# Both feed-forward layers of a transformer block as seven half products per pair of tiles, with weight sums formed by adding transfers

## The chip, the cores and the metric

The kernel runs on one core of a Trainium2 chip. Times are device microseconds (us) of one execution on that core. The engines are named as the profile names them: PE (matrix products), PEld (the loading of weights into PE, beside its products), DVE (vector), ACT (scalar, with its functions), POOL (general purpose) and SP, which here only starts transfers. SP, ACT and POOL each have a queue from which they issue DMA transfers. Every engine works through its own list of instructions in a fixed order; an instruction that waits holds up all that stand behind it on the same engine.

## What is computed

One block of a model on 640 tokens (128 context tokens, 512 latent ones), width 1024: a norm, two kinds of attention, an output projection, a second norm, a feed-forward net of hidden width 4096, and a last norm. The change touches the part from the second norm on:

```python
def _mlp(h, w_mlp_in, w_mlp_out):
    return jnp.square(jax.nn.relu(h @ w_mlp_in)) @ w_mlp_out
...
    x = x + g1 * _merge(a_o, b_o, ga, gb, w_br_a, w_br_b, w_out)
    h2 = _rmsnorm(x, n2) * (1 + sc2) + sh2
    x = x + g2 * _mlp(h2, w1, w2)
...
y_prompt = _rmsnorm(xp, final_norm_g)
```

The gates g, scales sc and shifts sh are a product of the conditioning vectors with a 1024 x 6144 matrix.

## The kernel before

Features lie on the 128 partitions, tokens along the free dimension: an activation is 8 tiles of 128 x 640, a weight tile is 128 output features by 1024 inputs (8 blocks of 128 x 128). Tokens are worked in two halves of 320. To keep float32 accuracy each operand is split into a high and a low part in a faster format: ACT writes the high part (a copy that rounds), DVE or POOL writes the low part (the difference). Each product is then three matmuls of 128 x 128 with 128 x 320: high by high, high by low, low by high (`gemm_k`, L339 to L341).

The hidden width is done in four chunks of 1024. In each chunk a first layer makes 8 hidden tiles (relu, then square, `relu2`, L1140 to L1150), and a second layer multiplies them with the chunk's 8 tiles of the second matrix and adds the result, scaled by the gate, to the residual tiles X1 (`add_gated`, L1100). A plain tile and token half takes 8 blocks x 3 = 24 matmuls. The first layer of chunk 0 and all second layers are plain. The first layers of chunks 1 to 3 take two weight tiles at a time as a 2 x 2 block matrix (input features 0 to 511 and 512 to 1023 by two tiles) and multiply it with the two token halves by seven products of half the depth, 12 matmuls each, in place of eight (`winograd`, L1204). The operands of the seven are the blocks A11, A12, A22 themselves and sums of blocks, S1 to S4, which DVE forms in SBUF (`raw`, L260) from two weight tiles that are held whole; ACT and DVE or POOL then split each (L280, L281). The sums on the activations' side, three sets T and a fourth that takes H2's place, are formed once from the normed input, in pieces between the products of chunk 0's second layer (`t_pieces`).

The order of DVE's list is that in which the program is written, from the merge before the output projection on (`manual_schedule`); those of PE, ACT, POOL and SP are set by the scheduler that builds the program. The output projection runs its last four tiles with the first token half ahead, so that the second norm of that half can run beside the second half's products. The norm's pieces are popped from the list `side` in the midst of and behind the products that follow: `rstd_half` (PE sums over the partitions, L174 and L175, then ACT, L176 and L177), then `norm2`, which scales (DVE, L360), shifts into the high part (ACT, L365) and makes the low part (DVE, L368). The second half's pieces run beside chunk 0's first products, which take the first token half of four weight tiles.

The gates, scales and shifts but the first norm's come from `late_mods`: 32 loads of 512 KB on POOL's queue (tiles wmt), and for each load four reductions on DVE (L992). `mod_pace` and `mod_step` put these between the products from the merge to chunk 0's first layer; the last eight loads, for the gates of the feed-forward net, come last.

## Time and profile before

| what | value |
|---|---|
| time, three runs | 1003.18, 1004.53, 1004.98 us (median 1004.53) |
| the profiled execution | span 1001.3 us, from the first to the last instruction; no time of its own is listed |
| feed-forward net in the profile | first product at 545.03 us, last at 991.27 us |
| ACT busy in 870 to 925 us (chunk 3, first layer) | 29.80 us of 55 |
| DVE busy in the same stretch | 40.55 us of 55 |

The profile's page counts the busy time of each engine over the span. Its other views list instructions in order of time, groups of like instructions with the mean duration of one and the wait ahead of it, busy times by stretches of the span, and transfers with the time from issue to landing. A matmul is listed with its whole passage through the array (0.31 us), which overlaps with the next one's; the distance between two starts is what one costs PE in a row of them.

### The profile page before, as it was taken

How to read it: one execution, taken by the hardware profiler on the slowest of the kernel's cores; microseconds unless marked ns; L12 is line 12 of the kernel's file. 1: busy time of each engine (PE TensorE's matmuls, PEld its weight loads, DVE VectorE, ACT ScalarE, POOL GpSimd, SP SyncE). 2: the span in 40 equal slices, each digit the busy share in tenths (PEclk: the TensorE clock that was granted, in tenths of full speed). 3: DMA queues.
4: the chain of work that ended last, by engine and by line, in shares of the span. 5: the costliest groups of instructions: out<-in, count | busy, mean ns of one | idle time of the engine just before them, and what ended most of it. 6: DMA issues, size and time to landing. Idle time of an engine off the chain costs nothing.

```text
span 1001.3 us, 16554 instructions
## 1 busy us (share of the span) xinstructions
...
## 2 busy tenths in 40 slices
...
GB/s 347 208 172 69 31 25 44 77 43 77 135 111 103 133 160 189 181 169 185 224 126 81 47 164 110 85 43 84 106 78 28 85 106 88 60 79 29 126 22 105
DMA packets 34767, 108.47 MB, mean 108 GB/s; under 512 B 4320, under 2 KB 8032, under 8 KB 34688
## 3 DMA queue, kind: packets, MB, share of 16 engines
...
## 4 chain that ended last, share of the span: by engine, by line
PE 65%; DVE 15%; ACT 8%; issue 3%; DMA 1%; POOL 0%; ACTq 0%; DVEq 0%; POOLq 0%; SPq 0%
PE pg L339 7%; PE pg L340 7%; PE pg L341 7%; PE pss L340 7%; PE pss L341 7%; PE pss L339 6%; PE pt L339 4%; PE pt L341 4%; PE pt L340 4%; DVE sr L260 3%; ACT wb L280 2%; PE pt L653 1%; PE pt L710 1%; DMA wst<-w 1%; DVE n L641 1%
## 5 line engine op out<-in xcount | busy, mean ns | idle before, releaser
L301 ACT ACTIVATE wh<-wst 128x1024 fp32r<-128x1024 f32 x84 | 88.8, 1057 | 112.4 <-PE pg L340 37.9
L302 DVE TENSOR_TENSOR wl<-wst,wh 128x1024 fp32r<-128x1024 f32 x53 | 64.8, 1223 | 67.5 <-ACT wh L301 67.4
L302 POOL TENSOR_TENSOR wl<-wst,wh 128x1024 fp32r<-128x1024 f32 x31 | 75.1, 2423 | 160.0 <-ACT wh L301 151.5
L992 DVE SCALAR_TENSOR_TENSOR mt<-wmt,cb 128x512 f32<-128x512 f32 x128 | 81.4, 686 | 0.0
L281 POOL TENSOR_TENSOR wb<-wst,wb 128x512 fp32r<-128x512 f32 x24 | 31.7, 1322 | 263.4 <-ACT wb L280 226.6
L339 PE MATMUL pss<-hidh,wh 128*128 128x320 f32 x216 | 67.0, 310 | 0.7 <-ACT hidh L1143 0.7
L340 PE MATMUL pss<-hidl,wh 128*128 128x320 f32 x216 | 67.0, 310 | 0.3
L341 PE MATMUL pss<-hidh,wl 128*128 128x320 f32 x216 | 66.7, 309 | 0.0
L607 DVE TENSOR_TENSOR pl<-pt,ph 128x512 fp32r<-128x512 f32 (+2 forms) x80 | 50.5, 633 | 18.3 <-ACT ph L606 17.3
L606 ACT ACTIVATE ph<-pt 128x512 fp32r<-128x512 f32 (+2 forms) x80 | 44.2, 555 | 28.8 <-PE pt L710 11.7
L280 ACT ACTIVATE wb<-sr 128x512 fp32r<-128x512 f32 x48 | 29.8, 627 | 51.5 <-DVE sr L260 35.6
L1150 DVE TENSOR_TENSOR hidl<-rl,hidh 128x320 fp32r<-128x320 f32 x64 | 37.5, 586 | 25.2 <-ACT hidh L1143 24.6
L988 POOL DMA_DIRECT2D wmt<-wmodB x32 | 17.1, 536 | 174.6 <-DVE mt L992 108.0
L340 PE MATMUL pg<-hidl,wh 128*128 128x320 f32 x144 | 44.7, 310 | 2.2 <-DVE hidl L1150 2.2
L281 DVE TENSOR_TENSOR wb<-sr,wb 128x512 fp32r<-128x512 f32 x48 | 36.0, 755 | 14.2 <-ACT wb L280 14.1
L339 PE MATMUL pg<-hidh,wh 128*128 128x320 f32 x144 | 44.7, 310 | 0.0
L341 PE MATMUL pg<-hidh,wl 128*128 128x320 f32 x144 | 44.5, 309 | 0.0
L340 PE MATMUL pt<-hidl,wh 128*128 128x320 f32 x136 | 42.1, 310 | 1.1 <-DVE hidl L1150 1.1
L341 PE MATMUL pt<-hidh,wl 128*128 128x320 f32 x136 | 42.0, 309 | 0.0
L339 PE MATMUL pt<-hidh,wh 128*128 128x320 f32 x136 | 42.0, 309 | 0.0
L644 ACT ACTIVATE pa<-pss,nm 128x320 f32<-128x320 f32 x64 | 33.1, 522 | 17.2 <-DVE nm L642 17.0
L339 PEld LDWEIGHTS pss<-hidh,wh 128*128 128x128 f32 x216 | 40.5, 188 | 1.5 <-ACT hidh L1143 1.5
...
## 6 DMA issues: line engine op xcount, KB each, us to landing
wst<-w SPq DMA_DIRECT2D x64, 512.0 KB, 3.6
wmt<-wmodB POOLq DMA_DIRECT2D x32, 512.0 KB, 4.2
wst<-w_in SPq DMA_DIRECT2D x31, 512.0 KB, 3.6
ms<-wmodA SPq DMA_DIRECT2D x16, 512.0 KB, 8.8
...
wst<-w_br SPq DMA_DIRECT2D x8, 512.0 KB, 4.4
wst<-w_out SPq DMA_DIRECT2D x8, 512.0 KB, 3.5
```

The source lines that it names most:

```text
L280: ACT.activation(t[:, lo4], src, AF.Copy)
L281: later.append(lambda: (nc.gpsimd if name in BLKP else DVE).tensor_sub(t[:, hi4], src, r32(t[:, lo4])))
L301: ACT.activation(hi, st, AF.Copy)
L302: (nc.gpsimd if key in WPOOLSET else DVE).tensor_sub(lo, st, r32(hi))
L339: PE.matmul(ps, wh[:, k], xh[:, sl], start=first, stop=False)
L340: PE.matmul(ps, wh[:, k], xl[:, sl], start=False, stop=False)
L341: PE.matmul(ps, wl[:, k], xh[:, sl], start=False, stop=last)
L606: ACT.activation(ph[:, :n], pt[:, :n], AF.Copy)
L607: DVE.tensor_sub(pl[:, :n], pt[:, :n], r32(ph[:, :n]))
L644: ACT.activation(p[:, HALVES[j]], ps[j][:, :HT], AF.Exp, bias=nm, accum_out=s2[:, j:j + 1])
L992: DVE.scalar_tensor_tensor(t, st[:, q * 512:(q + 1) * 512], 1.0, r32(cb[2 * q + i][:, :512]), op0=OP.mult, op1=OP.mult, accum_out=parts[:, ...
L1150: DVE.tensor_sub(dst[1][:, sl], r[:, :HT], r32(dst[0][:, sl]))
```

## The change

Both layers of all four chunks are done by seven products of half the depth. On the second layer the 2 x 2 blocks are the halves of the hidden features and two output tiles. A pair of weight tiles n (two tiles of 128 outputs) gives the seven products A11, A12, S3, S2, A22, S1, S4, each 12 matmuls (now L1386 to L1388); some of them add to one bank of PSUM: A12 goes on the bank of A11, S1 and S4 on that of S2, after what was there has been read.

- **Operands of the weights.** Whole weight tiles are loaded only for the A11 and A12 of chunk 0's first layer. All others come as blocks of 256 KB into 12 buffers `ra` (L1177, SP's queue). The sums are made by transfers that add into a buffer (`accum_op`, on POOL's queue): S3 is A21 with A11 added (L1179); S2, S4 and S1 come from S3 and A22 by one more addition each (L1203), issued when the operand before has been split from the same buffer. DVE's sums of blocks are gone. Six split operands can stand ready, as before.
- **Operands of the activations.** They are sets of four tiles, 128 x 1280, formed and split in one instruction per step (`form`, `split_set`). The normed input gives B11, B21 from the first token half (within `norm2`) and T3, T2, T4, T1, N22 once the second half is there. Each chunk's hidden tiles give the same seven for its second layer, into two buffers `op` that take turns.
- **Second layer.** Chunks 0 to 2 don't touch the residual. Each product's result is added to one of 28 sums `acc` (ACT copies in chunk 0, DVE adds in 1 and 2). In chunk 3 `fold` combines the sums and `reload` fetches the residual, which was stored to HBM before the net (`xd`), and adds the sums to it; chunk 3's own products are added one by one, and the last norm's squares are taken tile by tile (`done_half`).
- **Order.** DVE's list is hand-written only up to the end of the second norm; from there the scheduler sets it. Before the second half's norm all reductions of `late_mods` that are left are done (`mod_step(64 - lm_n[0])`), and their buffers are given back; the second norm is drained (`while side`) before the net's first product is written. PSUM is then laid out anew as 8 equal banks. The first products are A11 and A12 of two pairs at a time, which take the first token half only.

```diff
--- before.py
+++ after.py
...
-        def block(self, name, i):
...
-    if MAN:
-        ctx.enter_context(tc.manual_schedule(engines={(DVE.engine, ACT.engine, PE.engine)[i] for i in MAN}))
+    manual = ExitStack()
+    manual.enter_context(tc.manual_schedule(engines={DVE.engine}))
...
+    def split_set(t, src, ks=slice(0, 4), neg=False):
+        hi, lo = halves_of(t)
+        if neg:
+            ACT.activation(hi[:, ks], src[:, ks], AF.Copy, scale=-1.0)
+            DVE.scalar_tensor_tensor(lo[:, ks], src[:, ks], -1.0, r32(hi[:, ks]), op0=OP.mult, op1=OP.subtract)
+        else:
+            ACT.activation(hi[:, ks], src[:, ks], AF.Copy)
+            DVE.tensor_sub(lo[:, ks], src[:, ks], r32(hi[:, ks]))
+    def form(raw, name, tile_of, ks=slice(0, 4)):
+        c = {"B11": B11, "B21": B21, "N22": B22, "T4": B21}.get(name, B12)
+        b = [t[:, ks] for t in raw]
+        if name == "T3":
+            DVE.tensor_sub(b[B12], b[B22], b[B12])
+        elif name == "T2":
+            DVE.tensor_add(b[B12], b[B12], b[B11])
+        elif name == "T4":
+            DVE.tensor_sub(b[B21], b[B21], b[B12])
+        elif name == "T1":
+            DVE.tensor_sub(b[B12], b[B22], b[B12])
+        split_set(tile_of(name), raw[c], ks, name == "N22")
...
     def norm2(fs, h):
         mod_step(16 + 4 * (fs.stop + -fs.stop % MG) - lm_n[0])
-        modulate([(H2[f], X1[f], mod(2, f), mod(1, f)) for f in fs], rstd2, h)
+        off = HALVES[h].start
+        for f in fs:
+            for sl, g in SEGS[h]:
+                d = HR[2 * (f // 4) + h][:, f % 4, sl.start - off:sl.stop - off]
+                DVE.scalar_tensor_tensor(d, X1[f][:, sl], mod(2, f)[:, g:g + 1], rstd2[:, sl], op0=OP.mult, op1=OP.mult)
+                ACT.activation(d, d, AF.Identity, bias=mod(1, f)[:, g:g + 1])
+        if fs.stop % 4 == 0 and h == 0:
+            form(HR, ("B11", "B21")[fs.stop // 4 - 1], h2_set)
...
-        if n < KT - 4 or h == 0 and n < KT - 1:
+        if h or n < KT - 4:
             mod_pace(OU)
-        elif n == KT - 1:
+        if n == KT - 1:
+            if h == 0:
+                HR += [tt_pair("hr", F32).rearrange("p a (b n) -> p (a b) n", b=2) for _ in range(4)]
+            else:
+                mod_step(64 - lm_n[0])
             side += norm_pieces(acc2, sq, rstd2, h, lambda fs, h=h: norm2(fs, h))
-    def t_pieces(k):
...
-    def winograd(i, hid):
...
-    for c in range(4):
-        hid = [(v_tile("hidh"), v_tile("hidl")) for _ in range(KT)]
...
     while side:
         side.pop(0)()
+    for n in range(KT):
+        nc.sync.dma_start(xd[n], X1[n])
+    manual.close()
+    mod_pool.close()
...
+    for name in ("T3", "T2", "T4", "T1", "N22"):
+        form(HR, name, h2_set)
+    banks.close()
+    pp8 = ctx.enter_context(tc.tile_pool(name="pp8", bufs=1, space=bass.MemoryType.PSUM, reuse_waits="tile"))
...
+    m = open_phase("mlp", 0)
+    opt = [m.tile([P, 8, HT], F32R, tag="op", bufs=2, name="op")]
...
+    ORDER = ("A11", "A12", "S3", "S2", "A22", "S1", "S4")
+    def products():
+        for c in range(4):
+            late_ = []
+            if c == 0:
+                first = [(o, n) for i in (0, 2) for o in ORDER[:2] for n in (i, i + 1)]
+                for o, n in first + [(o, n) for o in ORDER[2:] for n in range(4)]:
+                    yield 1, c, n, o
+            else:
+                for n in range(4):
+                    yield 1, c, n, "S3"
+                    if n:
+                        yield 1, c, n - 1, "S1"
+                    yield 1, c, n, "A22"
+                    yield 1, c, n, "A11"
+                    if n:
+                        yield 1, c, n - 1, "S4"
+                    yield 1, c, n, "A12"
+                    yield 1, c, n, "S2"
+                late_ = [(1, c, 3, "S1"), (1, c, 3, "S4")]
+            for i, o in enumerate(ORDER):
+                for n in range(4):
+                    yield 2, c, n, o
+                    if i == 0 and n < len(late_):
+                        yield late_[n]
...
+        def load(self, x):
+            st, c, n, o = x
+            a = self.parts(st, c, n)
+            t = m.tile([P, 4, P], F32, tag="ra", bufs=NRA, name="ra")
+            nc.sync.dma_start(t, a["A21" if o == "S3" else o])
+            if o == "S3":
+                nc.gpsimd.dma_start(t, a["A11"], accum_op=OP.add)
...
+        def conv(self):
+            self.feed()
+            x = self.todo[self.n_conv]
+            st, c, n, o = x
+            src = {"S2": "S3", "S4": "S3", "S1": "A22"}.get(o, o)
+            t = self.raw[st, c, n, src]
+            w = wp.tile([P, KT, P], F32R, tag="w" + "hl"[self.n_conv % 2], bufs=3, name="wb")
+            ACT.activation(w[:, 0:4], t, AF.Copy)
+            (nc.gpsimd if o in BLKP else DVE).tensor_sub(w[:, 4:8], t, r32(w[:, 0:4]))
+            more = {"S3": "A22", "S2": "A12", "A22": "A21"}.get(o)
+            if more:
+                nc.gpsimd.dma_start(t, self.parts(st, c, n)[more], accum_op=OP.add)
+            else:
+                self.used -= 1
+                del self.raw[st, c, n, src]
+            self.t[x] = w
+            W.live += 1
+            self.n_conv += 1
+        def ahead(self):
+            while self.n_conv < len(self.todo) and W.live < 6:
+                self.conv()
+            self.feed()
...
+    def layer1(c, n, o, mm):
+        p = pairs.setdefault((c, n), Pair())
+        if c not in HID:
+            HID[c] = [m.tile([P, 4, HT], F32, tag=f"hid{i}", bufs=1, name=f"hid{i}") for i in range(4)]
+        hid = [t[:, n] for t in HID[c]]
+        if o in ("A11", "S3", "S2", "A22"):
+            p.__dict__["b" + o] = bank()
+        b = p.__dict__["b" + {"A12": "A11", "S1": "S2", "S4": "S2"}.get(o, o)]
+        mm(b, o not in ("A12", "S1", "S4"), o not in ("A11", "S2", "S1"))
+        if o == "A11":
+            p.pv = temp(c, "pv")
+            ACT.activation(p.pv, b, AF.Copy)
+        if o in ("A11", "S3") and hasattr(p, "pv") and hasattr(p, "bS3"):
+            p.w = temp(c, "w")
+            DVE.tensor_add(p.w, p.pv, p.bS3)
+        if o == "A12":
+            relu2(hid[B11], b)
...
+    def layer2(c, n, o, mm):
+        p = pairs.setdefault((c, n, 2), Pair())
+        if o in ("A11", "S3", "S2", "A22"):
+            p.__dict__["b" + o] = bank()
+        b = p.__dict__["b" + {"A12": "A11", "S1": "S2", "S4": "S2"}.get(o, o)]
+        mm(b, o not in ("A12", "S1", "S4"), o not in ("A11", "S2", "S1"))
+        if c == 0:
+            ACC[n, o] = half_tile("acc", 28)
+            ACT.activation(ACC[n, o], b, AF.Copy)
+            return
+        if c < 3:
+            DVE.tensor_add(ACC[n, o], ACC[n, o], b)
+            return
+        if o == "A11":
+            p.pv = half_tile("pv", 2) if n < 2 else half_tile("w", 2)
+            ACT.activation(p.pv, b, AF.Copy)
+            gated(XR[2 * n][:, HALVES[1]], p.pv, 2 * n, 3, 1)
+        elif o == "A12":
+            gated(XR[2 * n][:, HALVES[0]], b, 2 * n, 3, 0)
+            done_half(2 * n, 0)
...
+    def fold():
+        for n in range(4):
+            a = {o: ACC[n, o] for o in ORDER}
+            DVE.tensor_add(a["S3"], a["S3"], a["A11"])
+            DVE.tensor_add(a["A22"], a["A22"], a["S2"])
+            DVE.tensor_sub(a["A22"], a["A22"], a["S3"])
+            DVE.tensor_sub(a["S1"], a["S1"], a["S3"])
+            DVE.tensor_sub(a["S4"], a["A11"], a["S4"])
+    def reload():
+        for q in range(2):
+            t = hp_.tile([P, 4, NT], F32, tag="h", bufs=4, name="xr")
+            XR.extend(t[:, i] for i in range(4))
+        for n in range(KT):
+            nc.sync.dma_start(XR[n], xd[n])
+        neg = small("ng", 16, 1)
+        NG2.append(neg.rearrange("p (a b) -> p a b", b=2))
+        DVE.tensor_scalar(NG2[0], mods[:, 24:32], -1.0, None, op0=OP.mult)
+        for n in range(4):
+            gated(XR[2 * n][:, HALVES[0]], ACC[n, "A12"], 2 * n, 3, 0)
+        for n in range(4):
+            gated(XR[2 * n][:, HALVES[1]], ACC[n, "S4"], 2 * n, 3, 1)
+            gated(XR[2 * n + 1][:, HALVES[0]], ACC[n, "A22"], 2 * n + 1, 3, 0)
+            gated(XR[2 * n + 1][:, HALVES[1]], ACC[n, "S1"], 2 * n + 1, 3, 1)
...
+        def mm(ps, first, last_):
+            for k in range(4):
+                PE.matmul(ps, wh[:, k], xh[:, k], start=first and k == 0, stop=False, skip_group_check=True)
+                PE.matmul(ps, wh[:, k], xl[:, k], start=False, stop=False, skip_group_check=True)
+                PE.matmul(ps, wl[:, k], xh[:, k], start=False, stop=last_ and k == 3, skip_group_check=True)
+        (layer1 if st == 1 else layer2)(c, n, o, mm)
+        if early:
+            if o == "A12":
+                W.live -= 2
+        else:
+            W.live -= 1
+        OPS.ahead()
+        if st == 1 and o == "A12" and (n == 3 or c and n == 2):
+            form(HID[c], "B11", lambda q: opd(c, q), slice(0, 4) if c == 0 else slice(0, 3) if n == 2 else slice(3, 4))
...
+        if st == 2 and n == 3 and o in ORDER[:5]:
+            form(HID[c], {"A11": "T3", "A12": "T2", "S3": "T4", "S2": "T1", "A22": "N22"}[o], lambda q: opd(c, q))
+        if st == 1 and c == 3 and n == 0 and o == "S2":
+            fold()
+        if c == 3 and st == 1 and n == 3 and o == "S2":
+            reload()
...
-    nc = _bacc.Bacc("TRN2", target_bir_lowering=False, num_devices=1)
+    nc = _bacc.Bacc("TRN2", target_bir_lowering=False, num_devices=1, dynamic_dma_scratch_size=8192)
```

The text of the prediction speaks of three places. The first is DVE's list from the last residual addition of the output projection (L1021, the second half of tile x1_7, printed as x_7; L1100 before). `mt<-wmt` are the reductions of `late_mods` (L910 now, L992 before), `hr` the normed rows, `h2T` the first of the sums of activations. Before:

```order
L1100 SCALAR_TENSOR_TENSOR x_7_6439<-pt,parts,x_7_6439 128x320
L1150 TENSOR_TENSOR hidl<-rl,hidh 128x320 x2
L360 SCALAR_TENSOR_TENSOR xm<-x_0_6028,parts,rstd_6011 128x320
L360 SCALAR_TENSOR_TENSOR xm<-x_1_6097,parts,rstd_6011 128x320
L368 SCALAR_TENSOR_TENSOR hh0l<-xm,parts,hh0h 128x320
```

Now:

```order
L1021 SCALAR_TENSOR_TENSOR x_7_6402<-pt,parts,x_7_6402 128x320
L910 SCALAR_TENSOR_TENSOR mt,parts<-wmt,cb 128x512 x24
L889 TENSOR_TENSOR parts<-parts 128x16
L894 TENSOR_TENSOR parts<-parts,pk 128x16
L1075 SCALAR_TENSOR_TENSOR hr<-x_0_6005,parts,rstd_5996 128x320
```

Twenty-four reductions stand between the last residual addition and the second half's norm; before they stood in chunk 0, two at a time behind products.

The second place is ACT's list at the same point of the program, with the numbers of the buffers. L1038 and L1035 write high parts of sets, L1249 copies A11's result out of its bank, L1232 is the relu, L1199 splits a weight operand, L223 a whole weight tile. Now:

```order
L1076 ACTIVATE hr_6436<-hr_6436,parts_4353 128x320 x4
L1038 ACTIVATE h2T3_6725<-hr_6434 128x1280
L1038 ACTIVATE h2T2_6729<-hr_6434 128x1280
L1038 ACTIVATE h2T4_6733<-hr_6435 128x1280
L1038 ACTIVATE h2T1_6737<-hr_6434 128x1280
L1035 ACTIVATE h2N22_6740<-hr_6436 128x1280
L1249 ACTIVATE acc_6797<-b_6784 128x320
L1249 ACTIVATE acc_6812<-b_6799 128x320
L1249 ACTIVATE acc_6871<-b_6858 128x320
```

The copies of the first three A11 results stand behind the last of the seven sets; before, the relu of the first product stood ahead of the second half's norm in that list.

A few rows on, ACT's list now reads:

```order
L1199 ACTIVATE wb_6828<-ra_6752 128x512
L1232 ACTIVATE hid0_6780<-b_6799 128x320
L1199 ACTIVATE wb_6832<-ra_6755 128x512
L1233 ACTIVATE hid0_6780<-hid0_6780 128x320
L1199 ACTIVATE wb_6850<-ra_6758 128x512
L223 ACTIVATE wh_6873<-wst_6618 128x1024
```

The splits of the first three S3 operands (from `ra`) stand ahead of that of the fourth whole weight tile (wh_6873).

The third place is PE's list, where the third A11 product ends and the fourth product begins:

```order
L1386 MATMUL b_6858<-h2B11_6504,wh_6620 128x320
L1387 MATMUL b_6858<-h2B11_6504,wh_6620 128x320
L1388 MATMUL b_6858<-h2B11_6504,wl_6621 128x320
L1386 MATMUL b_6784<-h2B21_6564,wh_6529 128x320
L1387 MATMUL b_6784<-h2B21_6564,wh_6529 128x320
```

The fourth product is A12 of the first pair and goes on bank b_6784, that of the first A11, which the first of the three ACT copies reads; before, the second product took another bank (pg).

430 lines of the change are left out of this document (187 added, 243 removed).

## The prediction

> **What bounds the kernel now.** First the page: the span, and the shares of the chain that ended last.
>
> ```profile
> span 1001.3 us, 16554 instructions
> PE 65%; DVE 15%; ACT 8%; issue 3%; DMA 1%; POOL 0%; ACTq 0%; DVEq 0%; POOLq 0%; SPq 0%
> ```
>
> PE holds most of the chain. Then the busy times by stretches (columns: length; PE, PEld, DVE, ACT, POOL busy; PE's clock; DMA share; GB/s), in three places: beside the output projection, inside a layer of seven products, and over a layer change.
>
> ```profile
> 480.00:520.00 40.00, 40.00 (x275) 40.00 (x274) 25.77 (x51) 13.26 (x20) 11.19 (x7) 1.00 0.59 187
> 655.00:710.00 55.00, 55.00 (x377) 55.00 (x377) 46.18 (x82) 32.73 (x68) 9.82 (x9) 1.00 0.21 68
> 710.00:765.00 55.00, 53.55 (x360) 52.65 (x360) 25.18 (x42) 15.44 (x25) 5.69 (x3) 1.00 0.27 87
> ```
>
> Inside a layer PE never idles, so there time is the number of matmuls times their distance. The order of time on PE gives that distance, the edges of the net, and the few waits (in brackets: idle before, and what ended it).
>
> ```profile
> 519.76 0.31 PE L339 MATMUL pss<-mh,wh 128*128 128x320 f32 x1
> 519.91 0.31 PE L340 MATMUL pss<-ml,wh 128*128 128x320 f32 x1
> ...
> 531.64 0.70 PE L174 MATMUL pt<-acc,ones 128*128 128x320 f32 x2
> ...
> 545.03 0.31 PE L339 MATMUL pss<-hh0h,wh 128*128 128x320 f32 x1
> ...
> 550.27 0.41 PE L339 MATMUL pss<-hh6h,wh 128*128 128x320 f32 x1 [2.44 <-ACT hh6h L365]
> ...
> 552.57 0.64 PE L340 MATMUL pss<-hh6l,wh 128*128 128x320 f32 x1 [1.88 <-DVE hh6l L368]
> ...
> 553.26 0.47 PE L339 MATMUL pss<-hh7h,wh 128*128 128x320 f32 x1
> 553.53 0.47 PE L340 MATMUL pss<-hh7l,wh 128*128 128x320 f32 x1
> ...
> 718.72 0.41 PE L339 MATMUL pg<-hidh,wh 128*128 128x320 f32 x1
> 720.22 0.42 PE L340 MATMUL pg<-hidl,wh 128*128 128x320 f32 x1 [1.09 <-DVE hidl L1150]
> ...
> 991.42 0.70 PE L174 MATMUL pt<-acc,ones 128*128 128x320 f32 x2
> ```
>
> The distance is 0.1465 us (0.15 between the first two rows; 55.00 us for 377 matmuls in the window above is 0.146). Right after a wait it is 0.27 (553.26 to 553.53), the matmul then taking 0.47 instead of 0.31. The net has 384 matmuls in chunk 0's plain layer, 1536 in four plain second layers and 1008 in three layers of seven products: 2928, or 429 us of the 446.4 between 545.03 and 991.42. So all waits and slow stretches of the net are worth 17 us: about 8 at the start, and some 2 at each layer change (718.72 to 720.22 is one).
>
> **What goes.** All eight layers now take 4 pairs x 7 x 12 = 336, so 2688. The 240 that go are 35.2 us, if PE stays fed. That gain is sure; the rest is what PE waits for.
>
> **The change-over.** Up to the first half's norm the program is as before, so the axis of before serves until 533.95, when that half's scale is ready on ACT. What DVE must then do before PE can go past its first products is a chain, priced by these rows of time:
>
> ```profile
> 533.48 0.47 ACT L177 ACTIVATE rstd<-rstd 128x320 f32<-128x320 f32 x1
> ```
>
> ```profile
> 528.46 0.69 DVE L992 SCALAR_TENSOR_TENSOR mt<-wmt,cb 128x512 f32<-128x512 f32 x1
> 529.07 0.69 DVE L992 SCALAR_TENSOR_TENSOR mt<-wmt,cb 128x512 f32<-128x512 f32 x1
> ...
> 533.98 1.27 DVE L360 SCALAR_TENSOR_TENSOR xm<-x,parts,rstd 128x128 f32<-128x128 f32 x4 [3.22 <-ACT rstd L177]
> 535.17 0.68 DVE L368 SCALAR_TENSOR_TENSOR hh0l<-xm,parts,hh0h 128x128 fp32r<-128x128 f32 x2
> ...
> 537.44 0.49 DVE L169 TENSOR_TENSOR acc<-acc,sq 128x320 f32<-128x320 f32 x1 [0.54 <-ACT sq L167]
> ...
> 546.15 2.08 DVE L169 TENSOR_TENSOR acc<-acc,sq 128x320 f32<-128x320 f32 x1 [0.60 <-ACT sq L167]
> ...
> 555.61 0.54 DVE L1100 SCALAR_TENSOR_TENSOR x<-pt,parts,x 128x320 f32<-128x320 f32 x1
> ```
>
> and by these groups from 552 us on (count, then busy and mean ns, then idle before):
>
> ```profile
> L302 DVE TENSOR_TENSOR wl<-wst,wh 128x1024 fp32r<-128x1024 f32 x29 | 35.5, 1224 | 58.8 <-ACT wh L301 58.8
> L281 DVE TENSOR_TENSOR wb<-wst,wb 128x512 fp32r<-128x512 f32 x12 | 8.2, 685 | 0.0
> L360 DVE SCALAR_TENSOR_TENSOR xm<-x,parts,rstd 128x320 f32<-128x320 f32 x8 | 4.0, 546 | 1.9 <-ACT rstd L177 1.9
> L1209 DVE TENSOR_TENSOR cc<-pv,pss 128x320 f32<-128x320 f32 x20 | 9.6, 481 | 0.2
> L301 ACT ACTIVATE wh<-wst 128x1024 fp32r<-128x1024 f32 x35 | 37.0, 1056 | 66.3 <-PE pss L340 25.7 <-PE pg L340 24.4 <-PE pt L340 14.3
> L280 ACT ACTIVATE wb<-wst 128x512 fp32r<-128x512 f32 x36 | 22.0, 619 | 26.6 <-PE pss L340 11.8 <-PE pt L340 8.9 <-PE pg L340 6.0
> L1214 ACT ACTIVATE pv<-pg 128x320 f32<-128x320 f32 x8 | 3.4, 424 | 1.4 <-PE pg L1193 1.4
> ```
>
> Nothing in before is 1280 wide. From 512 to 1024 elements DVE goes from 0.685 to 1.224 and ACT from 0.619 to 1.056; carried on, a step of 1280 is an estimated 1.49 on DVE and 1.27 on ACT.
>
> 1. To the last residual addition: eight tiles' scaling 4.8 (1.19 for two, 533.98 to 535.17), four residual additions 2.2 (0.54), three square sums 1.5 (0.49) with waits of 0.6 for ACT's squares 1.8, six reductions 3.7 (0.61 apart), two lower parts of B11 and B21 3.0, two weight splits 2.4, waits for ACT's high parts and what is ahead of them in ACT's list 5.1 (an estimate: per set one shift, one high part, one square), and one instruction blocked for 1.6 more (2.08 against 0.49). Sum 26.1: DVE stands at **560**.
> 2. The 24 reductions at 0.61 are 14.6. Their loads have three buffers, so 0.3 of waits: **575**. Before, they lay two at a time beside products; here nothing covers them, since PE has only three A11 products to do.
> 3. Eight scalings of the second half 4.0 (**579**), then the operands: shift 0.42, T3's difference 1.49, ACT 1.27, T3 low 1.49, then T2, T4 and T1 with their differences and low parts, five steps of 1.49 = 7.45, ACT for T1 and for N22 2.54, and the A11 copy 0.42. Sum 15.1: **594**. In ACT's list the copies that free the A11 banks stand behind the last set, so the fourth product waits for all of it, though its operands need only the first half.
>
> PE's work from 531.64 to 594 is four output products (24 x 0.1465 each, 14.1), the norm's sums (2) and three A11 products (5.3): 41 us idle. In before the same stretch cost some 8.
>
> **The weights' start.** The buffers `ra` take the space that the normed rows give back, free with T1's low part at about 593.9. The prices of a transfer (issue; then KB each and median us to landing) and of POOL's splits behind it:
>
> ```profile
> L988 POOL DMA_DIRECT2D wmt<-wmodB x32 | 17.1, 536 | 174.6 <-DVE mt L992 108.0 <-DVE parts L972 37.3 <-PE pt L710 22.7
> ```
>
> ```profile
> wmt<-wmodB POOLq DMA_DIRECT2D x32, 512.0 KB, 4.2
> bkh<-bkh POOLq DMA_DIRECT2D x8, 224.0 KB, 5.9
> cb<-silu POOLq DMA_DIRECT2D x4, 256.0 KB, 3.7
> cos<-tabs SPq DMA_DIRECT2D x1, 256.0 KB, 4.0
> ```
>
> ```profile
> 545.47 2.41 POOL L302 TENSOR_TENSOR wl<-wst,wh 128x1024 fp32r<-128x1024 f32 x1 [3.83 <-ACT wh L301]
> ```
>
> ```profile
> L281 POOL TENSOR_TENSOR wb<-wst,wb 128x512 fp32r<-128x512 f32 x24 | 31.7, 1322 | 263.4 <-ACT wb L280 226.6
> ```
>
> No row of before shows an adding transfer. Its ends are 3.7 us (plain, same size, same queue) and, since it must fetch the old sum too, two plain ones after each other, 8; I take 5, between 3.7 and the 5.9 of the slowest queue-mate. So the first S3 lands at 593.9 + 4.0 + 0.5 + 5 = 603.4, the third a microsecond later. ACT's list puts three S3 splits ahead of the fourth whole tile, so its high part starts at 604.4 + 0.6, takes 1.06, and POOL's low part 2.4: **608.5**. PE has three A12 products meanwhile (to 599.3): 9 us more idle. The ends are 2 (sums at once, only the split shows) and 15. After such a pause PE runs at the slow distance; the stretch behind 553 cost 3.3 (28 matmuls at 0.12 more), and I take that.
>
> The Trainium skill (Collectives: The Full Stack, "The bandwidth ceiling: the fold count and why AG ≠ RS ≠ AR") holds that a reducing transfer is slow for its second source read and not for the addition, which makes it half as fast as a copy. By that a 256 KB sum would cost what 512 KB cost, for which the row above has 4.2 us, and the total would be 0.8 lower; no run here shows it yet.
>
> **The net after that.** 2616 matmuls are left: 383.2 us. Beside them, per layer of 49.2 us (336 x 0.1465):
> - Transfers: 16 plain and 16 adding ones of 256 KB. At 187 GB/s for a share of 0.59 (window at 480) the engines do 317 GB/s, 0.83 us each: 13.3 for the plain, 13.3 to 26.6 for the others. It fits. A sum has from one split of a buffer to the next about 12 us of products, against 5 to 8.
> - DVE in chunks 1 and 2's second layers: 20 splits of 0.685, nine 1280-wide steps of 1.49, 28 sums of 0.48, in all 40.5. It fits.
> - Layer changes: of seven, some have late products of the layer before as cover; I price three at 2.3 as before's, 7 in all.
> - Chunk 3: `fold` puts 20 x 0.42 = 8.4 on DVE in one piece, `reload` 24 scaled additions, 8.8. Six split operands ready are 10.5 us of cover, partly used: 4 each, 8 (0 if the cover holds, 17 if none is left).
> - The last second layer: 20 x 0.685 + 9 x 1.49 + 44 x 0.48 + 12 x 0.49 = 54 of DVE against 49.2 of PE, with each tile's squares waiting for ACT: 15 (5 if only the surplus shows).
>
> So waits of 30 (12 to 45). The tail is before's, 1001.3 - 991.4 = 9.9.
>
> **Sum**: 608.5 + 3.3 + 383.2 + 30 + 9.9 = 1034.9 on the profiled execution's axis, whose span was 1001.3; the median of the runs is 3.2 above that span. **1038 us**: 35 saved, some 47 lost at the start (41 + 9 + 3 against 6 to 8), some 21 later (30 against 9).
>
> **Rivals.**
> - *Adding transfers are dear.* If one occupies the engines three times as long as a plain one, a layer needs 16 x (0.83 + 2.49) = 53 us of them against 49.2, and PE waits for S2, S1 and S4 everywhere; with landings of 12 us or more the chain S3, S2, S4 falls behind by itself. Eight layers at 4 to 9 more give 1070 to 1110, at centre **1088**. For: nothing in before bounds it; 5.9 us for 224 KB on that queue. Against: 3.7 and 4.2 for plain ones. Chance 0.24.
> - *The change-over is short*, the one on the other side: if the scheduler's list lets PE start its A12 products before the second half's operands (the copies done early), or the reductions run beside output products, the idle time at the start falls below about 8 us more than today's; the gain of 35 then outweighs chunk 3 and the total is **986**. It decides from a start idle under 25 us. Against: both lists show the copies and the reductions where I priced them. Chance 0.06.
> - *DVE becomes the bound.* POOL splits 64 operands now; blocking as in the 2.08 row at each of a layer's 8 would add 8 x 1.3 = 10.6 to 40.5, past 49.2: 2 a layer and 6 in the last, so 1044 to **1058**. It lies within the range; part of the forecast's 0.63.
> - *Little wait in chunk 3 and quick sums*: 1000 to 1012; 0.07.
>
> The Trainium skill (SBUF — State Buffer, "Who interferes with whom") says that a DVE instruction with two inputs in SBUF and a POOL instruction that reads SBUF exclude each other for a whole instruction, the first to issue winning. The trace agrees: 2.08 at 546.15 beside a POOL split from 545.47 to 547.88, against 0.49 alone.
>
> **How the numbers follow.** Forecast 0.63 (1012 to 1060), dear transfers 0.24, little wait 0.07, short change-over 0.06. The range 1012 to 1092 leaves out the last two and the upper part of the second. 0.2% is about what a measurement of this kernel can tell from no change: faster 0.06, same 0.02 (inside the third case), slower 0.92.
>
> **What would show it.** PE idle 41 us in all between 531.64 and its fourth product, with DVE in a row of 24 reductions of which the last ends near 575; copies of A11 on ACT near 594; the first S3 landing some 9.5 us behind T1's low part; waits of PE in chunk 3 that name `fold`'s and `reload`'s results or weight splits behind them; adding transfers at 5 us. I am wrong if PE's idle time at the start is under 25 us, or if PE waits for S2, S1 or S4 operands inside every layer.

## The result and the profile after

The changed kernel takes **1050.91 us** (median of four runs, 1048.20 to 1060.32) against 1004.75 us before (1003.18 to 1005.43). The ratio is **1.0481**, with a 95% interval of 1.0436 to 1.0527: slower by nearly 5%, 13 us above the forecast and inside its range. The profiled execution took 1049.26 us, its span is 1047.5.

The page of the changed kernel first: its span, then the shares of the chain that ended last, by engine.

```profile
span 1047.5 us, 16807 instructions
...
PE 44%; DVE 20%; DMA 12%; ACT 7%; issue 6%; POOL 4%; POOLq 0%; SPq 0%; DVEq 0%; ACTq 0%
```

Before, PE held 65% of that chain and transfers 1%. Now transfers hold 12%, and POOL, which held nothing, 4%. So matmuls behind matmuls set less of the end, and something that goes over transfers has come on the path.

The windows of the changed kernel (columns as in the prediction) show where: two at the change-over from the output projection to the net, one shortly behind it, one from the last products of chunk 0's second layer over chunk 1's first, and one from the end of chunk 2 over chunk 3's first layer to the change to its second.

```profile
545.00:575.00 30.00, 9.69 (x40) 8.10 (x40) 26.07 (x74) 7.22 (x15) 2.15 (x4) 0.64 0.40 138
575.00:595.00 20.00, 2.41 (x9) 2.41 (x10) 15.69 (x16) 10.33 (x15) 0.00 (x0) 0.50 0.07 22
605.00:615.00 10.00, 5.28 (x18) 4.88 (x19) 4.65 (x4) 3.99 (x7) 5.83 (x5) 0.50 0.90 196
700.00:750.00 50.00, 48.25 (x328) 47.78 (x327) 24.94 (x38) 28.62 (x57) 22.70 (x23) 1.00 0.72 159
905.00:985.00 80.00, 69.50 (x433) 67.98 (x432) 53.69 (x96) 38.38 (x77) 32.46 (x30) 0.91 0.68 167
```

In the first two windows, 50 us, PE works for 12 and DVE for 42: the change-over is DVE's. From 700 to 750 PE misses less than 2 us. From 905 to 985 it misses 10 of 80, and there the DMA engines are busy for 0.68 of the time, against 0.27 in before's window at 710.

The order of time on PE, changed kernel, gives the waits at the change-over (idle before in brackets) and one of chunk 3.

```profile
555.85 1.44 PE L177 MATMUL pt<-acc,ones 128*128 128x320 f32 x2 [12.24 <-DVE acc L172]
559.17 1.43 PE L178 MATMUL pt<-sq,ones 128*128 128x320 f32 x2 [1.89 <-ACT sq L170]
...
592.59 0.64 PE L1386 MATMUL b<-h2B,wh 128*128 128x320 f32 x1 [25.16 <-ACT acc L1249]
...
609.69 0.63 PE L1386 MATMUL b<-h2B,wh 128*128 128x320 f32 x1 [9.11 <-ACT wh L223]
...
969.97 0.55 PE L1386 MATMUL b<-op,wb 128*128 128x320 f32 x1 [4.07 <-ACT op L1038]
```

Adding such rows up for the whole net gives the balance of the case. The table counts, for each profiled execution, every gap between two matmuls beyond their distance of 0.1465 us: as a wait above 0.2 us, as slow distance from 0.06 to 0.2. In the changed kernel the three stretches are about the second norm with chunk 0's first layer (520 to 660 us), the net up to the end of chunk 2 (660 to 905), and chunk 3 with the last norm; the borders stay the same for all, so a faster kernel has part of chunk 3 ahead of 905. All numbers are in us, worked out from the rows of PE in order of time; the kernels of the experiments are explained below. The table is steadier than the spans, in which the stages ahead of the net differ by up to 6 us from one execution to another (the wait of 12.24 us above, the same in most kernels here, ends between 553.9 and 559.7). But it is of one execution each: the changed kernel, e1, e2, e4 and e5 run the same instructions between 660 and 905 and wait there for 10.8 to 15.8 us, so 5 us in that column are not told from none.

The slow distance goes with the clock that is granted to PE: in the window from 605 to 615 it is 0.50 of full speed, and the matmuls from 610 on are 0.27 us apart. Some 12 of the changed kernel's 15 us of slow distance lie where the granted clock is 0.5.

| kernel | median | ratio to before (95%) | waits to 660 | 660 to 905 | past 905 | slow distance |
|---|---|---|---|---|---|---|
| before | 1004.75 | 1 | 6.0 | 4.2 | 3.7 | 3.4 |
| changed | 1050.91 | 1.0481 (1.0436 to 1.0527) | 52.8 | 10.8 | 22.0 | 15.2 |
| e1_spread | 1054.53 | 1.0501 (1.0471 to 1.0530) | 49.6 | 14.4 | 22.1 | 15.6 |
| e2_raearly | 1050.50 | 1.0448 (1.0407 to 1.0490) | 49.4 | 15.0 | 20.3 | 11.7 |
| e3_plain | 1023.47 | 1.0178 (1.0147 to 1.0208) | 50.8 | 0 | 13.2 | 8.4 |
| e4_chunk3 | 1057.47 | 1.0517 (1.0477 to 1.0556) | 53.6 | 15.8 | 20.3 | 16.1 |
| e5_short | 1046.79 | 1.0461 (1.0386 to 1.0536) | 49.3 | 14.1 | 20.2 | 14.7 |
| e6_pool_order | 1035.15 | 1.0301 (1.0259 to 1.0342) | 55.0 | 1.9 | 17.7 | 9.8 |
| e7_s3_plain | 1039.56 | 1.0351 (1.0315 to 1.0388) | 51.3 | 7.0 | 18.4 | 11.6 |
| e8_s2_dve | 1060.03 | 1.0557 (1.0520 to 1.0593) | 53.7 | 22.8 | 18.3 | 19.5 |
| e9_no_pool_split | 1038.65 | 1.0327 (1.0288 to 1.0367) | 52.8 | 4.6 | 17.0 | 11.7 |
| e10_all | 1014.47 | 1.0093 (1.0069 to 1.0118) | 40.1 | 0 | 15.3 | 9.1 |
| e11_all_plain | 1004.23 | 0.9999 (0.9978 to 1.0019) | 32.6 | 0 | 11.3 | 9.0 |
| e12_all_short | 1007.57 | 1.0032 (1.0013 to 1.0051) | 30.8 | 0 | 14.1 | 8.4 |

From before to changed, waits and slow distance rise from 17.3 to 100.8, by 83.5 us; the 240 matmuls that went give back 35.2; 48.3 is left, and the spans differ by 46.2. 50 of the 83 are lost up to 660 (46.8 in waits, 3.3 in the slow distance of that stretch), the rest between layers, in chunk 3 and at the end.

### The profile page after: what moved, and what is told of

It reads as the page before. It is cut to its first block, busy times and chain, and to the rows that moved or that the text cites. A ratio compares the mean times of both kernels' runs of the same rounds, so it can differ in the third digit from the quotient of the medians.

```text
span 1047.5 us, 16807 instructions
## 1 busy us (share of the span) xinstructions
PE 934.6 (89%) x6077; PEld 883.8 (84%) x6077; DVE 753.9 (72%) x1574; ACT 574.6 (55%) x1210; POOL 319.1 (30%) x310
## 4 chain that ended last, share of the span: by engine, by line
PE 44%; DVE 20%; DMA 12%; ACT 7%; issue 6%; POOL 4%; POOLq 0%; SPq 0%; DVEq 0%; ACTq 0%
DMA ra<-w 11%; PE pg L255 4%; PE pg L256 4%; PE b L1386 4%; PE pg L257 4%; PE b L1387 4%; PE b L1388 4%; PE pss L256 3%; PE pss L255 3%; PE pss L257 3%; DVE wb L1200 2%; POOL wb L1200 2%; PE pt L256 2%; PE pt L257 2%; PE pt L255 2%
## 5 line engine op out<-in xcount | busy, mean ns | idle before, releaser
L1199 ACT ACTIVATE wb<-ra 128x512 fp32r<-128x512 f32 x216 | 134.1, 627 | 144.0 <-DMA ra<-w 81.4
L1200 DVE TENSOR_TENSOR wb<-ra,wb 128x512 fp32r<-128x512 f32 x156 | 124.8, 802 | 94.3 <-ACT wb L1199 93.4
L1386 PE MATMUL b<-op,wb 128*128 128x320 f32 x448 | 139.9, 313 | 11.4 <-ACT op L1038 10.0
L1387 PE MATMUL b<-op,wb 128*128 128x320 f32 x448 | 140.5, 314 | 6.2 <-DVE op L1039 6.1
L1388 PE MATMUL b<-op,wb 128*128 128x320 f32 x448 | 139.1, 311 | 0.0
L255 PE MATMUL pg<-h,wh 128*128 128x320 f32 x352 | 112.5, 320 | 1.0 <-ACT qrs L453 0.6
L1200 POOL TENSOR_TENSOR wb<-ra,wb 128x512 fp32r<-128x512 f32 x60 | 94.7, 1591 | 59.5 <-ACT wb L1199 51.8
L256 PE MATMUL pg<-h,wh 128*128 128x320 f32 x352 | 110.5, 314 | 0.0
L257 PE MATMUL pg<-h,wl 128*128 128x320 f32 x352 | 110.1, 313 | 0.0
L1203 POOL DMA_DIRECT2D ra<-w x96 | 85.4, 909 | 70.2 <-DVE wb L1200 45.3
L1386 PEld LDWEIGHTS b<-op,wb 128*128 128x128 f32 x448 | 84.6, 189 | 13.5 <-ACT op L1038 11.3
L1387 PEld LDWEIGHTS b<-op,wb 128*128 128x128 f32 x448 | 84.8, 189 | 8.9 <-DVE op L1039 8.3
L1386 PE MATMUL b<-h2T,wb 128*128 128x320 f32 x256 | 82.5, 322 | 5.4 <-DVE x L1257 5.4
L1388 PEld LDWEIGHTS b<-op,wb 128*128 128x128 f32 x448 | 84.8, 189 | 0.4 <-POOL wb L1200 0.3
L1387 PE MATMUL b<-h2T,wb 128*128 128x320 f32 x256 | 82.0, 320 | 0.0
L1388 PE MATMUL b<-h2T,wb 128*128 128x320 f32 x256 | 82.0, 320 | 0.0
L910 DVE SCALAR_TENSOR_TENSOR mt<-wmt,cb 128x512 f32<-128x512 f32 x128 | 80.7, 684 | 0.0
L223 ACT ACTIVATE wh<-wst 128x1024 fp32r<-128x1024 f32 x50 | 52.9, 1058 | 45.1 <-PE pg L256 14.6
L255 PEld LDWEIGHTS pg<-h,wh 128*128 128x128 f32 x352 | 66.9, 190 | 5.1 <-ACT raw L730 2.8
L256 PEld LDWEIGHTS pg<-h,wh 128*128 128x128 f32 x352 | 66.9, 190 | 1.5 <-issue 0.2
```

What stands on the lines that cost most here:

```text
L223: ACT.activation(hi, st, AF.Copy)
L255: PE.matmul(ps, wh[:, k], xh[:, sl], start=first, stop=False)
L256: PE.matmul(ps, wh[:, k], xl[:, sl], start=False, stop=False)
L257: PE.matmul(ps, wl[:, k], xh[:, sl], start=False, stop=last)
L910: DVE.scalar_tensor_tensor(t, st[:, q * 512:(q + 1) * 512], 1.0, cb[2 * q + i][:, :512], op0=OP.mult, op1=OP.mult, accum_out=parts[:, q, n ...
L1199: ACT.activation(w[:, 0:4], t, AF.Copy)
```

## The experiments

All are edits of the changed kernel, and every gain or loss below is against it unless said otherwise. Its own runs spread over 12 us, so a difference of medians of 4 us is not told from none; there the waits decide.

### The change-over: reductions earlier

In this kernel two half steps of the reductions (four reductions) stand behind each of the first twelve products of the output projection, in place of the pacing rule.

```diff
-        if h or n < KT - 4:
-            mod_pace(OU)
+        if n < KT - 4 or h == 0:
+            mod_step(2)
```

> The reductions that are left at the end of the output projection are done inside it instead: two steps (four reductions) behind each of its first twelve products. Theory (DVE's chain after the last residual addition sets when PE goes on): the fourth product of the net, 25.2 us late now, starts 12 to 15 us earlier (24 x 0.61 = 14.6), PE's waits behind it stay, total 1036 to 1039. Rival (DVE has no room earlier: the same work in the projection holds up PE's residual sums there): PE waits appear before the net, the fourth product moves by 5 us or less, total 1045 to 1051. Rival (the first sums of weights set it): the 9.1 us wait for the fourth weight tile grows by what is saved, total unchanged.

Measured: 1054.53 us, and the fourth product (A12 of the first pair) starts at 593.0, where it started before the edit. The rows of PE in that kernel:

```profile
544.35 1.41 PE L177 MATMUL pt<-acc,ones 128*128 128x320 f32 x2 [8.55 <-DVE acc L172]
...
569.52 1.44 PE L177 MATMUL pt<-acc,ones 128*128 128x320 f32 x2 [12.41 <-DVE acc L172]
...
593.02 0.64 PE L1386 MATMUL b<-h2B,wh 128*128 128x320 f32 x1 [12.71 <-ACT acc L1249]
```

The 25 us before the fourth product became 12.7, and what went from there stands earlier, before the norm's sums. DVE's rows of the same kernel say why: a square sum, of which there is one for each output product, comes every 4.0 to 4.1 us.

```profile
526.94 0.49 DVE L172 TENSOR_TENSOR acc<-acc,sq 128x320 f32<-128x320 f32 x1 [0.54 <-ACT sq L170]
530.95 0.49 DVE L172 TENSOR_TENSOR acc<-acc,sq 128x320 f32<-128x320 f32 x1 [0.60 <-ACT sq L170]
```

PE's product takes 24 x 0.1465 = 3.5 us. With four reductions behind each product DVE sets the pace of the projection, so this order makes PE wait there as much as it saves later. A sparser one was not run. It may have room: in the changed kernel DVE stands idle for 7 us between 521 and 533, in waits for PE's products (1.75 and 1.77 the longest) and for the first half's norm (3.23).

### The change-over: reductions shortened

The last 24 reductions work on 64 of their 512 elements.

```diff
-                    DVE.scalar_tensor_tensor(t, st[:, q * 512:(q + 1) * 512], 1.0, cb[2 * q + i][:, :512], op0=OP.mult,
+                    DVE.scalar_tensor_tensor(t[:, :L], st[:, q * 512:q * 512 + L], 1.0, cb[2 * q + i][:, :L], op0=OP.mult,
```

> The last 24 reductions sum 64 of their 512 elements, so that their place and loads stay and some 13 us of DVE's time go (24 x 0.55); the gates of the feed-forward net come out otherwise. Theory (DVE's chain sets when PE goes on; moving the reductions earlier gave nothing because the products there take 3.5 us and the additions, squares and four reductions behind each 4.1 us): the fourth product starts 11 to 13 us earlier against the third, and since the weights' loads hang on T1 the whole rest moves with it: total 1036 to 1040. Rival (the loads of the reductions or the sums of weights set it): less than 5 us, total above 1045.

Measured: 1046.79 us. PE of that kernel:

```profile
587.63 0.64 PE L1387 MATMUL b<-h2B,wh 128*128 128x320 f32 x1 [20.44 <-ACT acc L1250]
```

The fourth product comes 5 us earlier, less than the 10 that DVE saved: by DVE's groups in this kernel the 24 reductions take 4.0 us in place of 14.6, but wait 5.6 for their loads of 512 KB, which have three buffers. So right behind DVE's work stand the loads, and a cure for one alone brings half. The time gained 4 us, within the spread.

### The change-over: the first sums of weights issued earlier

The hidden tiles of chunk 0 are allocated ahead of the weight buffers `ra`, so that these don't lie on the space of the normed rows.

```diff
+    HID[0] = [m.tile([P, 4, HT], F32, tag=f"hid{i}", bufs=1, name=f"hid{i}") for i in range(4)]
     OPS.ahead()
```

> The four hidden tiles of chunk 0 are laid out ahead of the ra buffers, so that the ra buffers lie where the projection's inputs were (free early) and not where the normed rows are. Theory (the loads start late because of their place, and ACT's list holds the fourth tile behind the splits of S3): the first S3 lands before PE needs it, the 9.1 us wait before the fourth pair's A11 falls to 1 to 3 us, total 6 to 8 us shorter: 1043 to 1045. Rival (adding transfers or POOL's queue are slow by themselves at that point): S3 still lands 10 us behind T1, no change.

Measured: 1050.50 us. The rows of POOL (first below) and of PE in that kernel:

```profile
566.90 3.58 POOL L1179 DMA_DIRECT2D ra<-w  x4
```

```profile
595.41 0.63 PE L1387 MATMUL b<-h2B,wh 128*128 128x320 f32 x1 [28.30 <-ACT acc L1249]
...
604.39 0.42 PE L1387 MATMUL b<-h2B,wh 128*128 128x320 f32 x1 [1.11 <-ACT wh L223]
```

The sums are issued at 567 in place of some 595, and the second wait falls from 9.11 to 1.11. The first one grew by 3 (25.16 to 28.30), because DVE's list came later: one of the 24 reductions waits for its load, which none does in the changed kernel.

```profile
568.78 0.69 DVE L910 SCALAR_TENSOR_TENSOR mt<-wmt,cb 128x512 f32<-128x512 f32 x1 [2.70 <-DMA wmt<-wmodB]
```

That the weights' loads and sums, which now run beside it, held this load up is likely, but not shown. The waits between the layers, 15.0 against 10.8, are within what kernels with the same instructions there differ by. The prediction's cause of the 9 us, the buffers' space, is shown; a gain in time is not.

### The sums: plain transfers in their place

All 128 adding transfers become plain ones of the same block: the same instructions, queue, bytes and buffers, with the sums left out.

```diff
-                nc.gpsimd.dma_start(t, a["A11"], accum_op=OP.add)
+                nc.gpsimd.dma_start(t, a["A11"])
...
-                nc.gpsimd.dma_start(t, self.parts(st, c, n)[more], accum_op=OP.add)
+                nc.gpsimd.dma_start(t, self.parts(st, c, n)[more])
```

> All adding transfers become plain ones of the same size on the same queue, so that the weights are the blocks last loaded and not the sums; the output differs. Theory (adding costs about as much again as a plain transfer on the engines, but it fits under a layer): landing falls from 4.9 to about 3.7 us, the share of POOL's queue from 27% to about 17%, the total by 2 to 8 us, most of it at the start and at the change into chunk 3's second layer: 1043 to 1049. Rival (adding transfers set the pace): total falls by 20 us or more, below 1031.

Measured: 1023.47 us, 27 less. PE's waits between 660 and 905 are gone, those past 905 fell from 22.0 to 13.2, the slow distance from 15.2 to 8.4; at the start 2 us went. So nearly all of the sums' cost lies **behind the start, in the net**, where the prediction held them hidden; of the two readings on record the rival holds. The views show what differs. Transfers of the changed kernel (KB each, median us from issue to landing), then its POOL queue (packets, MB, share of 16 engines' span):

```profile
ra<-w POOLq DMA_DIRECT2D x128, 256.0 KB, 4.9
ra<-w SPq DMA_DIRECT2D x120, 256.0 KB, 3.5
```

```profile
q0 software_dynamic: 24896, 57.04, 27.0%
```

The same two views with plain transfers:

```profile
ra<-w POOLq DMA_DIRECT2D x128, 256.0 KB, 3.1
ra<-w SPq DMA_DIRECT2D x120, 256.0 KB, 3.1
```

```profile
q0 software_dynamic: 16704, 57.04, 18.2%
```

And of the kernel before, without these 128 transfers:

```profile
q0 software_dynamic: 6464, 23.47, 8.1%
```

In time of all 16 engines the queue holds 282.8 us (27.0% of 1047.5), 186.0 with plain transfers (18.2% of 1022.2) and 81.1 before. One plain transfer is (186.0 - 81.1) / 128 = 0.82 us, an adding one (282.8 - 81.1) / 128 = 1.58: **1.92 times** as much, for 1.8 us more to landing. The rule from the Trainium skill (Collectives: The Full Stack, "The bandwidth ceiling: the fold count and why AG ≠ RS ≠ AR") that the prediction weighed, that a reducing transfer is half as fast as a copy for its second source read, agrees with this ratio; the landing of 4.9 us is longer than the 4.2 that the prediction worked out by it. The 0.82 us is also what the prediction took for a plain one (0.83).

Yet 128 x 0.76 us more of engine time isn't 27 us of the kernel by itself: the engines were busy for 0.75 of the time between 612 and 905. (Besides, a plain transfer holds POOL for 545 ns to issue where an adding one takes 909; the 27 us are the worth of all these differences together.) The chain of waits of the changed kernel, over a layer change, shows what turns 1.8 us into a wait.

```profile
738.19 0.70 DVE wb L1200
738.91 4.47 DMA ra<-w
743.45 0.48 issue
743.98 0.51 POOL ra L1179
744.53 7.72 DMA ra<-w
752.34 0.63 ACT wb L1199
...
753.74 0.42 ACT hid L1232
...
755.06 0.48 ACT op L1038
755.58 0.64 PE b L1386
```

DVE's low part frees a buffer at 738.9; the first block of an S3 is loaded into it (4.47 us, SP's queue); only then can POOL issue the addition, which takes 7.72 to land; ACT splits it, and behind that split stand the relu and the operand set of the next layer, for which PE waits. From the freed buffer to the split are 13.4 us. Who waits for what, in the changed kernel between 612 and 1040 us (total us, times, longest), on ACT and then on POOL:

```profile
ACT wb L1199 <- DMA ra<-w: 72.1, 34, 6.4
```

```profile
POOL ra L1179 <- DMA ra<-w: 57.6, 16, 10.3
```

The 57.6 us are time in which POOL stands at the addition of an S3 whose first block has not landed; every other addition and every split that is behind it in POOL's list waits with it. That gave three readings to tell apart: it is the S3 (a chain of two transfers), the order of POOL's list, or the load of splits on POOL.

### The sums: only those of S3 plain

The edit is the first of the two lines above alone.

> Only the 32 first sums (S3) become plain transfers of the same size on the same queue; the 96 others still add; the output differs. All 128 plain gave 1023, 27 us less. Theory 1 (S3's chain of a freed buffer, a load and a sum at each change of layer): most of it, 15 to 25 us less, 1026 to 1036. Theory 2 (the turns of S2 and S1 in the second layers, four operands or 7.0 us apart, against 0.6 for ACT, 0.7 to 1.6 for the low part, 0.9 for the issue and 4.9 for landing): 4 to 10 us less, 1041 to 1047. Theory 3 (the engines' time, as 1.58 us of one sum against 0.81): a quarter of 27, 7 us, 1044.

Measured: 1039.56 us, 11 less, with a quarter of the sums taken away: between what the first two theories gave. ACT's waits for transfers didn't fall (78.3 us against 72.1). So the S3 chain is a part of the cause, not the whole.

### The sums: another order on POOL

POOL's list follows the program's order, and the addition of S3 is written 8 operands ahead of its use, so that its first block has more time to land.

```diff
+        def adds(self):
+            while self.pend and self.pend[0][0] <= self.n_conv + 8:
+                i, t, src = self.pend.pop(0)
+                nc.gpsimd.dma_start(t, src, accum_op=OP.add)
...
-                nc.gpsimd.dma_start(t, a["A11"], accum_op=OP.add)
+                self.pend.append((self.todo.index(x), t, a["A11"]))
...
+    ctx.enter_context(tc.manual_schedule(engines={nc.gpsimd.engine}))
     OPS.ahead()
```

> POOL's list from the net on is that of the program, with S3's adding transfer put eight operands ahead of its split instead of right behind the first block's load. Theory 1 (POOL waits in order for first blocks to land, 57.6 us in all, and other sums and splits stand behind it): that wait falls below 20 us, PE's waits at the changes of layer fall by half, total 6 to 12 us shorter: 1039 to 1045. Theory 2 (the chain from a freed buffer over load and sum to the split is too long in itself, and POOL's place in it is short): total within 4 us of 1051.

Measured: 1035.15 us, 16 less. Every sum is still made, and lands no sooner (5.3 us). Waits on ACT and POOL in that kernel, same window:

```profile
ACT wb L1206 <- DMA ra<-w: 68.4, 45, 3.5
```

```profile
POOL ra L1171 <- DMA ra<-w: 32.7, 8, 10.9
```

ACT waits as long as before in all (68.4 against 72.1), but in 45 pieces of at most 3.5 us in place of 34 of up to 6.4. POOL stands at S3's additions for 32.7 us in place of 57.6. PE's waits from 660 to 905 fall from 10.8 to 1.9, which fits six operands that stand ready and cover short pieces but not long ones. So **the order of an in-order list** is worth 16 us: not what a sum costs, but what stands behind it while it waits. Whether these 16 are part of the 27 this run alone can't tell; e11 below bears on it.

### The sums: S2 by DVE

S2 is formed from S3 and A22 by an addition on DVE in place of a transfer. The sums stay the same.

```diff
-            more = {"S3": "A22", "S2": "A12", "A22": "A21"}.get(o)
+            more = {"S2": "A12", "A22": "A21"}.get(o)
...
+                DVE.tensor_add(t3, t3, self.raw[st, c, n, "A22"])
```

> S2 is formed by DVE (S3's buffer plus A22's, 128x512), not by an adding transfer; 32 adding transfers go and DVE gets 32 additions of 0.69. A22 must be loaded by then, some operands earlier. Theory 2 of the run before (turns too short): ACT's waits for S2 in the second layers (9.4 us of 72) go, total 5 to 10 us shorter: 1041 to 1046. Theory 3 (the engines' time): 32 x 1.58 of 51 us per engine go, total about 8 us shorter, waits for S1 and S3 fall too. Rival (buffers: A22 held longer makes the loads of S3 later): waits at the changes of layer grow, total 1048 to 1056.

Measured: 1060.03 us, 9 more. ACT's waits for transfers fell to 42.7 us, as intended, but PE's from 660 to 905 rose to 22.8. The same view of that kernel:

```profile
POOL ra L1179 <- DMA ra<-w: 76.4, 16, 11.3
```

POOL stands still for longer at S3's additions (76.4 us against 57.6). That fits the rival on record: A22 must now be loaded before S2 can be made, so it holds one of the 12 buffers longer and other loads start later. The buffers were not varied alone, so this cause is argued. Fewer sums were in any case not faster.

### The sums: no splits on POOL

All lower parts of weight operands go to DVE.

```diff
-BLKP = ('A12', 'A22')
+BLKP = ()
```

> The low parts of A12 and A22, 60 of 128x512 on POOL, are made by DVE; POOL's list in the net is then adding transfers alone. POOL's order is the scheduler's, as after the change. Theory (what a sum waits for is POOL's list: a first block's landing, and splits that wait for ACT; POOL's splits and DVE's also block each other, 1.57 us of a split against 0.80): ACT's 72 us of waits for sums fall below 45, PE's waits in the net by 10 to 20 us, total 1030 to 1040, although DVE gets 60 x 0.69 = 41 us more. Rival (DVE becomes the bound, 40.5 + 8 x 0.69 of 49.2 us per layer and waits on ACT): PE's waits for DVE's results grow, total 1050 to 1060.

Measured: 1038.65 us, 12 less. The groups of the changed kernel (count; busy and mean ns; idle before), then of this one:

```profile
L1200 DVE TENSOR_TENSOR wb<-ra,wb 128x512 fp32r<-128x512 f32 x156 | 124.8, 802 | 94.3 <-ACT wb L1199 93.4
...
L1200 POOL TENSOR_TENSOR wb<-ra,wb 128x512 fp32r<-128x512 f32 x60 | 94.7, 1591 | 59.5 <-ACT wb L1199 51.8
...
L1203 POOL DMA_DIRECT2D ra<-w x96 | 85.4, 909 | 70.2 <-DVE wb L1200 45.3
```

```profile
L1200 DVE TENSOR_TENSOR wb<-ra,wb 128x512 fp32r<-128x512 f32 x216 | 150.3, 698 | 82.3 <-ACT wb L1199 81.5
```

60 splits of 1.59 us leave POOL, and DVE pays only 25.5 us for them (150.3 against 124.8), because each of its own 156 became shorter by 0.1 us with no split on POOL beside it. ACT's waits for transfers fall from 72.1 to 40.9 us, as the theory had it, in which POOL, free of splits, reaches its additions sooner.

### Chunk 3 in pieces

`fold` is done in four pieces behind the first products of chunk 3, and `reload`'s scaled additions next to the product that needs each.

```diff
-        if st == 1 and c == 3 and n == 0 and o == "S2":
-            fold()
+        if st == 1 and c == 3 and n < 2 and o in ("A11", "S2"):
+            fold(2 * n + (o == "S2"))
```

> fold in four pieces, one after each of four products of chunk 3's first layer, and the scaled additions of reload next to the second-layer products that use them, with its loads where they were. Theory (DVE in one piece holds up the splits of weights and the sums there): the 2.8 us wait at 923 us goes, the waits of 4.1 and 2.0 us at 966 to 972 us fall to 2 or less together, later waits grow by some 2 us, total 4 to 8 us shorter: 1043 to 1047. Rival (these waits come from the change of layer, as at the earlier ones): waits stay within 1 us, total 1049 to 1052.

Measured: 1057.47 us; waits past 905 of 20.3 against 22.0. At the last layer change PE waits twice. The first wait is what it was (4.07 in the changed kernel), the second is shorter:

```profile
974.47 0.63 PE L1385 MATMUL b<-op,wb 128*128 128x320 f32 x1 [4.26 <-ACT op L1038]
975.93 0.64 PE L1386 MATMUL b<-op,wb 128*128 128x320 f32 x1 [0.83 <-DVE op L1039]
```

Rows of ACT, DVE and PE in the changed kernel tell the two apart.

```profile
966.72 0.63 ACT L1199 ACTIVATE wb<-ra 128x512 fp32r<-128x512 f32 x1 [6.43 <-DMA ra<-w]
...
970.28 1.14 DVE L1021 SCALAR_TENSOR_TENSOR xr<-acc,parts,xr 128x128 f32<-128x128 f32 x3 [1.62 <-DMA xr<-xd]
...
972.48 0.64 PE L1387 MATMUL b<-op,wb 128*128 128x320 f32 x1 [1.97 <-DVE op L1039]
```

Ahead of the first wait stands a split that waited 6.43 us for its transfer, with the relu and the operand set behind it in ACT's list. Ahead of the second stands `reload`: DVE waits for the stored residual to land, and the low part of the operand set is behind these additions in its list. With the additions elsewhere, 1.97 became 0.83. With plain transfers, and `fold` and `reload` in one piece (e3), the first wait falls to 0.72, but the second is there still:

```profile
949.78 0.64 PE L1387 MATMUL b<-op,wb 128*128 128x320 f32 x1 [3.14 <-DVE op L1039]
```

So the larger waits in chunk 3's middle belong to the sums; the one of 2.84 at 926 too, which stays here (3.58) and is gone with plain transfers. The smaller one is `reload`'s, through its loads.

### All together

This kernel has POOL's order and S3's lead, no splits on POOL and chunk 3 in pieces. It also starts differently: the normed rows have a pool of their own, so the buffers `ra` are free early; A11 and A12 of chunk 0 take a bank each and are added by DVE, so that all eight of these products run before any other operand; and T3 is formed first, with the splits of S3 behind it, T2 and the rest after that.

```diff
-BLKP = ('A12', 'A22')
+BLKP = ()
...
-                first = [(o, n) for i in (0, 2) for o in ORDER[:2] for n in (i, i + 1)]
+                first = [(o, n) for n in range(4) for o in ORDER[:2]]
...
+        own = c == 0 and o in ("A11", "A12")
...
+                def add(d=hid[B11](), v=p.pv, b=b):
+                    DVE.tensor_add(d, v, b)
+                    relu2(d, d)
+                deferred.append(add)
...
+        if x == (1, 0, 0, "S3"):
+            form(HR, "T3", h2_set)
+            for _ in range(4):
+                OPS.conv()
+            form(HR, "T2", h2_set)
...
```

> All that the runs before point to: POOL's list is the program's, S3's sum is put eight operands ahead, no splits on POOL (as in the run beside it); the normed rows lie in a pool of their own, so that the sums' buffers come free before them; chunk 0's A11 and A12 have a bank each, A12's result is added by DVE, and all eight products and the splits of S3 stand ahead of T2, T4, T1 and N22; chunk 3's additions in pieces. Theory: e6's 16 us and the 10 to 20 of POOL's splits are partly the same (20 to 25 together), the eight early products and earlier sums take 12 to 18 us off the start: 1050 - 35 to 43 = 1007 to 1015. Rival (the start is DVE's list as a whole, so early products only move the wait): 1022 to 1030. Better than before only if both are at their best, below 1002.

Measured: 1014.47 us, 36 less than the changed kernel and still 0.9% over the one before. PE in that kernel:

```profile
559.74 1.44 PE L179 MATMUL pt<-acc,ones 128*128 128x320 f32 x2 [12.24 <-DVE acc L174]
...
592.12 0.63 PE L1439 MATMUL b<-h2T,wb 128*128 128x320 f32 x1 [15.03 <-ACT wb L1212]
```

No wait is left between 660 and 905. At the start 40 us remain of 53, and 15 of 22 in chunk 3 and at the end. Two kernels ask what these are.

First, the same kernel with plain transfers:

> The kernel of e10_all with every adding transfer replaced by a plain one of the same block (the sums of weight blocks are left out; the same instructions run). In the changed kernel the same edit took 27 us. Theory (order and buffers, not the transfers themselves, cost the 27): in e10_all the splits' waits for transfers are already down from 72 to 27 us and few of them reach PE, so 2 to 8 us go: 1006 to 1012 us. Rival (an adding transfer costs what it costs wherever it stands): 15 to 27 us go, 988 to 1000 us.

Measured: 1004.23 us, 10 less, between the two theories and nearer to the first. The waits name the places: 7.5 us at the start, none from 660 to 905, 4.0 past 905. From 660 to 905 PE waits in neither kernel, so there the sums now cost it nothing; at the start, in chunk 3 and at the end they still do. With POOL's order, its splits and the start mended the sums are thus worth 10 us in place of 27, so most of the 27 hung on what stood around them.

Second, the same kernel with the last 24 reductions, and their loads too, cut to 64 of 512 elements:

> The kernel of e10_all with the last 24 reductions of the gates over 64 of their 512 elements, and only these elements loaded (left out: the rest of those sums). Theory (DVE's list between the two halves of the norm sets the start, and the reductions are its largest piece): 24 reductions of 0.61 us become some 0.12 to 0.2, so 10 to 12 us go and, without the load they wait for and without the addition of 4.31 us beside POOL's split, up to 15: 1000 to 1005 us, about what the kernel before takes. Rival (the first sums of weights, which wait for their buffers, set the start, as the loads did in e5_short): under 5 us go, 1010 us or more.

Measured: 1007.57 us, 6.9 less, below the theory's 10 to 15 and above the rival's 5; the waits to 660 fall by 9.3. The row that answers to the one at 592.12:

```profile
578.98 0.64 PE L1440 MATMUL b<-h2T,wb 128*128 128x320 f32 x1 [5.61 <-ACT wb L1213]
```

So the uncovered reductions with their loads make 9 us of what is left at the start, but 30.8 us of its waits stay without them. Neither kernel, with work left out, is faster than the one before. A version that beats it was not found.

## Why the prediction was right, point by point

**The gain.** 35.2 us for 240 matmuls: the balance of the table, with this gain in it, misses the difference of the spans by 2 us.

**The change-over, 41 us idle.** Confirmed step by step. The last residual addition stands at 558.07 on DVE, on an axis that is 1.6 us behind that of before, so at 559.7 for the forecast 560. The 24 reductions end at 573.4, the eight scalings took 3.78 for 4.0. The rows on DVE behind them, changed kernel:

```profile
573.74 3.78 DVE L1075 SCALAR_TENSOR_TENSOR hr<-x,parts,rstd 128x320 f32<-128x320 f32 x8
...
578.15 1.49 DVE L1046 TENSOR_TENSOR hr<-hr 128x1280 f32<-128x1280 f32 x1 [0.54 <-ACT hr L1076]
580.98 1.49 DVE L1039 TENSOR_TENSOR h2T<-hr,h2T 128x1280 fp32r<-128x1280 f32 x1 [1.33 <-ACT h2T L1038]
```

The 1280-wide step, carried on from 512 and 1024 elements, was estimated at 1.49 and is 1.49. The fourth product starts at 592.59, 594.2 on before's axis, for 594; the idle time up to there is 12.24 + 1.89 + 25.16 = 39.3. The price was right because the list was priced as it stands, with the copies of A11 on ACT behind the seventh set.

**The weights' start, 9 us: in part luck.** 9.11 in the row at 609.69, and e2 shows its cause, the buffers' space. The adding transfer's 5 us to landing, taken between 3.7 and 5.9, are right for the median of all 128 (4.9), but not here, where the forecast used them. Between 592 and 604 us four sums are issued beside twelve loads, and land after

```profile
ra<-w POOLq DMA_DIRECT2D x4, 256.0 KB, 9.7
```

So the wait ends at 611.3 on before's axis, not at 608.5. It is no longer than forecast because PE comes to it later too (602.2, not 599.3): the three A12 products ran for the most part at the slow distance, which the prediction put behind the wait. With the slow distance the start cost 50 us more than before, for some 46.

**The net after that: the step that failed.** Waits and slow distance past 660 are 42.3 us, against the 30 that the prediction gave its waits, and 8.9 before. Nearly all the 13 us of error lie here, and that they are no more is luck: two errors stand against each other. With plain transfers in place of the sums (e3) the same stretches hold 17 us (13.2 of waits, 3.9 of slow distance). So all but the sums, priced at 30, took 17, and the sums, put at nothing here, took 25:

- "A sum has from one split of a buffer to the next about 12 us of products, against 5 to 8." In a second layer the order is four S3, four S2, four A22, four S1, so from S3 to S2 and from A22 to S1 of the same pair are four products, 7.0 us, while split, low part, issue and landing take 0.6 + 0.7 to 1.6 + 0.9 + 4.9 = 7.1 to 8.0. What was worse, the sum's own first block waits for a buffer (the chain of 13.4 us), and POOL's list holds other work behind it. The sums were counted as hidden in the layers and cost some 25 us there and in chunk 3 (e3).
- "POOL splits 64 operands now" (60 by the profile), priced at a few blocked instructions, stood as a rival within the range. Taking the splits away is worth 12 us (e9). DVE's busy time grew with that by 25.5 us, and ACT's waits for transfers fell by 31, so the cost lay in POOL's own list more than in DVE's blocked instructions.
- "Chunk 3 ... 4 each, 8": waits of that size are there, 2.84 at 926 and 4.07 at 970, but they stay with `fold` and `reload` in pieces (e4) and shrink or go with plain transfers (e3). Only the 1.97 behind them are `reload`'s. A right number for a reason that is mostly wrong.
- The last layer was priced at 15; its waits in the changed kernel are some 10.

**The rivals.** *Dear transfers* had the right place and a wrong mechanism: the engines had room (1.92 times a plain transfer, not 3), and it was the chain of a freed buffer, a load, an addition and a split, each in some in-order list, that fell behind. PE's own rows from 660 to 905 name no weight operand as the end of a wait, but sets of activations and additions that read a bank. Its price, 50 us over the forecast, was twice what the sums took in the layers. *The change-over is short* would have needed under 25 us of idle time there; it was 39.3. *DVE becomes the bound* was meant of the layers, and there it doesn't hold: DVE took on 25.5 us of splits and the kernel became faster (e9).

**What stays open.** Open are the 30.8 us at the start that the last reductions don't explain (e12), among them the 12.24 us wait for the norm's square sums, which no kernel here shortened, and the waits in chunk 3 and at the end that are left without the sums (11.3 us in e11). Whether a version with chunk 0's first layer left as before, whose plain products covered the second half's norm, would beat both kernels was not tried, nor were the reductions put inside chunk 0, whose load buffers lie where the sums of weights now are.
